# Attention with bias on one core: k and q transposed by the DMA engines, V in a ring of five pairs

## The chip, the core and the metric

The kernel runs on one core of a Trainium2 chip. Its engines work side by side, each with its own queue of instructions: PE (TensorE, matmuls and weight loads), DVE (VectorE), ACT (ScalarE), POOL (GpSimd) and SP (SyncE). Here POOL issues the loads and SP the stores. 16 DMA engines move the data for all queues. The metric is device time in microseconds (us); a run is one execution, and the time given is the median of several.

## What is computed

q, k and v are float32 arrays of shape 4 x 8 x 1024 x 64 (batch, heads, sequence, head dimension), the bias is 1 x 1 x 1024 x 1024 and is shared by all heads:

```python
scale = 1.0 / np.sqrt(head_dim)
scores = scale * np.matmul(q, k.transpose(0, 1, 3, 2))
scores = scores + bias
scores_max = np.max(scores, axis=-1, keepdims=True)
attn = np.exp(scores - scores_max) / (np.sum(np.exp(scores - scores_max), axis=-1, keepdims=True) + 1e-8)
return np.matmul(attn, v)
```

That is 32 heads, each with 1024 x 1024 scores, so 33.5 million exponentials.

## The kernel before

**Pairs, banks and groups.** Two heads make a pair, and there are 16 pairs (`NP`). A sequence of 1024 is cut into 8 chunks of 128 keys (`kc`) and two halves of 512 queries (`qh`). A *bank* is one block of transposed scores, 128 keys by 512 queries of one head; a pair has 32. `banks` (L113 to L146) is the order of all banks, in which the late banks of one half are mixed with the early banks of the next. Six banks are left out of that order (`dgroups`, L138 to L141): their exponential is computed on DVE in steps (`d_steps`, L205). All others are taken three at a time as a *group* (`slots`, L149): one activation of 128 x 1536 elements.

**The way of a bank.** `s_fill` (L165) writes a group's scores into a PSUM buffer `ps`, of which there are two: one matmul a bank (L172), with the transposed keys `kT` as weights and the transposed queries `qT` as the moving operand. Both heads share one `kT`: head 0 lies in partitions 0 to 63 and head 1 in 64 to 127, so `qT` holds each head's queries with zeros in the other half. `s_exp` (L178) takes the group through ACT's exp into a tile `E`. The bias comes in by multiplication on DVE with exp(bias), `eb` (`mul_pair`, L235); for the last two key chunks of the second query half it is added on PE instead, by a matmul with the identity (L176, the *late bias*), from `braw`, which DVE copies out of PSUM (L255). `av_bank` (L261) multiplies `E` with V and a column of ones into a small PSUM tile `po` (L269), over the 8 banks of one half of one head; then DVE takes the reciprocal of the sums (L279), scales (L281), and SP stores (L289).

**Loads and transposes.** `load_qk` (L75) loads k and q of a pair from HBM on POOL's queue, with a cast from float32 to bfloat16, into `kr` and `qr` (three buffers each). `load_v` (L82) loads V of a pair in two DMAs into `vall`, which holds all 16 pairs. `transpose_pe` (L86) transposes k or q on PE, 16 small transposes for a whole pair (L92), into a PSUM tile `px`; DVE then copies kT (L107) or multiplies qT with `mask`, which makes the zeros (L102). `kT` and `qT` have three buffers each (`kvp`). The tiles `px`, `po` and two others (`pd` and the late bias) share the two buffers of `ps_x`, named xa and xb.

**What sets the order.** Pair 0 is started by an order written out by hand (L324 to L404): the loads of pairs 0, 1 and 2, V of pairs 0 and 1 and the bias in four parts. The rest is laid out by a planner that runs when the program is built. It keeps a modelled time for ACT, DVE and PE, with a cost for each kind of work (`EXP`, `QK`, `AV`, `MUL`, `EVAC`, L409 to L410), and appends to each engine the piece of work that could start first. `pe_fill`, `pe_piece`, `pe_d` and `pe_av` offer work for PE, `dve_pick` for DVE from `dve_q`, a list of (due time, priority, cost, work), and `act_pick` for ACT. `raw_at` (L422) holds the times at which the planner believes that k and q of a pair have landed; it sets 26.0 and 28.5 us for pair 2, and 7 us from the issue for later pairs (L537). `pieces` (L424 to L429) lists the transposes of pairs 1 to 15; the one of q of a pair issues the loads of k and q three pairs on and of V two pairs on (L534 to L539). Within an engine the instructions then run in the order in which they were appended, and wait on semaphores for data and buffers.

Of the kernel before, what the change touches and what calls it, by code (L numbers as in the profile page):

```python
# [9 lines left out]
BF = mybir.dt.bfloat16  # L10
# [6 lines left out]
def kernel(  # L17
# [15 lines left out]
    nc = tc.nc  # L33
    B, H, S, D = q.shape
    P = 128
# [27 lines left out]
    eb = consts.tile([P, 2, NCH, HQ], BF)  # L63
    braw = consts.tile([P, 2, HQ], BF)
    mask = consts.tile([P, 2, HQ], BF)
    vall = consts.tile([P, 2 * NP, NCH, D1], BF)

    k0f = consts.tile([P, 2, QC, D], F32)
    q0f = [consts.tile([P, QC, D], F32, name=f"q0f{t}") for t in range(2)]
# [11 lines left out]

    def load_v(pr):  # L82
        for t in range(2):
            nc.gpsimd.dma_start(out=vall[:, 2 * pr + t, :, :D], in_=vf[pr, :, t])  # L84

    def transpose_pe(pr, which, c0, n, tag):  # L86

        src = raws[pr][which]
        px = ps_x.tile([P, n, P], BF, tag=tag, name="px")
        for c in range(n):  # L90
            for t in range(2):
                nc.tensor.transpose(px[t * D:(t + 1) * D, c, :], src[:, t, c0 + c, :], ident[:])  # L92
        if (pr, which) not in trs:
            trs[(pr, which)] = (kvp.tile([P, NCH, P], BF, name="kT") if which else
                                kvp.tile([P, 2, NCH * P], BF, name="qT"))
        dst = trs[(pr, which)]

        def copy():
            if which == 0:

                m = n // QC
                nc.vector.tensor_tensor(  # L102
                    dst[:, :, c0 * P:(c0 + n) * P].rearrange("p t (m q) -> p t m q", m=m),
                    px.rearrange("p (m c) q -> p m (c q)", m=m).unsqueeze(1).to_broadcast([P, 2, m, HQ]),
                    mask.unsqueeze(2).to_broadcast([P, 2, m, HQ]), op=ALU.mult)
            else:
                nc.vector.tensor_copy(dst[:, c0:c0 + n, :], px[:])  # L107
        return copy


    NE = NCH - 2
    DPR = (3, 7, 11)
# [52 lines left out]
    def s_fill(g):  # L165
        if ("S", g) not in open_ps:
            open_ps[("S", g)] = ps_s.tile([P, 3, HQ], F32, tag="s", name="ps")
        ps = open_ps[("S", g)]
        for j, b in enumerate(slots[g]):
            pr, h, qh, kc = banks[b]  # L170
            qT, kT = trs[(pr, 0)], trs[(pr, 1)]
            nc.tensor.matmul(ps[:, j, :], kT[:, kc, :], qT[:, h, qh * HQ:(qh + 1) * HQ],  # L172
                             start=True, stop=b not in late_bias)
        for j, b in enumerate(slots[g]):
            if b in late_bias:
                nc.tensor.matmul(ps[:, j, :], ident[:], braw[:, late_bias[b], :], start=False, stop=True)  # L176

    def s_exp(g):  # L178
        n = len(slots[g])
        nc.scalar.activation(e_at(slots[g][0], n), open_ps.pop(("S", g))[:, :n, :], ACTF.Exp, scale=scale)  # L180
# [6 lines left out]
    LOG2E = 1.4426950408889634  # L187

    def d_fill(b, tag):
        pr, h, qh, kc = banks[b]  # L190
        ps = ps_x.tile([P, HQ], F32, tag=tag, name="pd")
        nc.tensor.matmul(ps[:], trs[(pr, 1)][:, kc, :], trs[(pr, 0)][:, h, qh * HQ:(qh + 1) * HQ], start=True, stop=False)  # L192
        nc.tensor.matmul(ps[:], ident[:], braw[:, late_bias[b], :], start=False, stop=True)  # L193
        d = d_of[b][0]
        if d not in dtiles:
            dtiles[d] = {"y": dp.tile([P, 2, HQ], I32, name="dy"), "f": dp.tile([P, 2, HQ], F32, name="df"),
                         "p": dp.tile([P, 2, HQ], I16, name="dpw"),
                         "b": dp.tile([P, 2, HQ], F32, name="db"), "e": de.tile([P, 2, HQ], BF, name="de")}

        def fixed():  # L200
            nc.vector.tensor_scalar(dtiles[d]["y"][:, d_of[b][1], :], ps[:], scale * LOG2E * 65536.0, 127.0 * 65536.0,  # L201
                                    op0=ALU.mult, op1=ALU.add)
        return fixed
# [57 lines left out]
    def av_bank(b, tag):  # L261
        pr, h, qh, kc = banks[b]
        first, last = (b == units[pr, h, qh][i] for i in (0, -1))
        if first:
            po[h] = ps_x.tile([P, QC, D1], F32, tag=tag, name="po")
        acc = po[h]
        e = e_at(b, 1)
        for i in range(QC):
            nc.tensor.matmul(acc[:, i, :], e[:, 0, i * P:(i + 1) * P], vall[:, 2 * pr + h, kc, :],  # L269
                             start=(first and i == 0), stop=last, skip_group_check=True)  # L270
        if not last:
            return None

        def evac():
            if qh == 0:
                oalls[h] = op.tile([P, NCH, D], F32, tag=f"o{h}", name="oall")
            oall = oalls[h]
            rs = small.tile([P, QC, 1], F32, name="rs")
            nc.vector.reciprocal(rs[:], acc[:, :, D:D1])  # L279
            c0 = qh * QC  # L280
            nc.vector.tensor_tensor(oall[:, c0:c0 + QC, :], acc[:, :, :D],  # L281
                                    rs[:].to_broadcast([P, QC, D]), op=ALU.mult)
# [13 lines left out]
    def av_last(x, bs, tag):  # L296
        first = len(last_left[x]) == 8
        if first:
            po[x] = (ps_x if tag != "s" else ps_s).tile([P, M, D1], F32, tag=tag, name="po")
        acc = po[x]  # L300
        for b in bs:
            last_left[x].remove(b)
        for i in range(M):
            for b in bs:
                nc.tensor.matmul(acc[:, i, :], e_at(b, 1)[:, 0, (x * M + i) * P:(x * M + i + 1) * P],
                                 vall[:, 2 * NP - 1, banks[b][3], :], start=first and i == 0 and b == bs[0],
                                 stop=not last_left[x] and b == bs[-1], skip_group_check=True)
        if last_left[x]:
            return None

        def evac():
            oh = small.tile([P, M, D], F32, name=f"oh{x}")
            rs = small.tile([P, M, 1], F32, name=f"rh{x}")
            nc.vector.reciprocal(rs[:], acc[:, :, D:D1])
            q = (nc.scalar, nc.sync)[x]
            if x == 0:
                for i in range(M):
                    nc.scalar.activation(oh[:, i, :], acc[:, i, :D], ACTF.Copy, scale=rs[:, i, :])
            else:
                nc.vector.tensor_tensor(oh[:], acc[:, :, :D], rs[:].to_broadcast([P, M, D]), op=ALU.mult)  # L320
            q.dma_start(out=of[2 * NP - 1][:, QC + x * M:QC + (x + 1) * M, :], in_=oh[:])
        return evac

    with tc.manual_schedule():  # L324
# [10 lines left out]
        kr0 = raw.tile([P, 2, NCH, D], BF, name="kr")  # L335
        raws[0] = (qr0, kr0)
        kT0 = kvp.tile([P, NCH, P], BF, name="kT")
        qT0 = kvp.tile([P, 2, NCH * P], BF, name="qT")
        trs[(0, 0)], trs[(0, 1)] = qT0, kT0

        nc.gpsimd.memset(qT0[D:, 0, :HQ], 0.0)
# [53 lines left out]
        for x in range(2):  # L395
            for y in range(2):
                nc.vector.memset(mask[x * D:(x + 1) * D, y, :], 1.0 if x == y else 0.0)
        s_exp(2)
        load_v(0)
        nc.gpsimd.dma_start(out=btraw[:, QC:QC + 2, :], in_=bf_[:, QC:QC + 2, :])  # L400
# [21 lines left out]
        raw_at = {0: (5900, 12600), 1: (19600, 20900), 2: (26000, 28500)}  # L422
        PM = 2
        pieces = [(0, 0, QC, QC)]  # L424
        for pr in range(1, NP):
            if pr < PM:
                pieces += [(pr, 1, 0, QC), (pr, 0, 0, QC), (pr, 1, QC, QC), (pr, 0, QC, QC)]
            else:
                pieces += [(pr, 1, 0, NCH), (pr, 0, 0, NCH)]  # L429
# [66 lines left out]
        def pe_piece():  # L496
# [23 lines left out]
            def emit(t):  # L520
# [5 lines left out]
                def run(t2):  # L526
# [7 lines left out]
                    if pr < NP and which == 0 and c0 + n == NCH:  # L534
                        if pr + 3 < NP:
                            load_qk(pr + 3)
                            raw_at[pr + 3] = (t2 + 7000, t2 + 7000)  # L537
                        if pr + 2 < NP:
                            load_v(pr + 2)  # L539
                dve_q.append((t + pe_cost(t, cost_t) + SEM, 0, cost, run))  # L540
            return ready, cost_t, emit

# [4 lines left out]
        def act_bank():  # L547
            i = min(len(filled), NO - 1)
            while order[i][0] != "S":
                i -= 1  # L550
            return slots[order[i][1]][0]

        def pe_d():
            if not d_todo:
# [172 lines left out]

        while len(act_end) < NO or av_next < NA or any(last_left) or dve_q:
            c = []
            a, d, p = act_pick(), dve_pick(), pe_pick()  # L730
            if a:
                c.append((a[0], 0))
# [62 lines left out]
```

## Time and profile before

| | |
|---|---|
| median of 3 runs | 246.78 us (245.88 to 246.88) |
| profiled execution: its own time | 248.31 us |
| profiled execution: span from first to last instruction | 246.5 us |
| mean granted TensorE clock | 0.993 |
| DMA: mean rate | 97 GB/s, 23.80 MB in 48752 packets |

The profile is that of one execution. In its lines, an instruction is named by its line in the kernel, its engine and operation, and what it writes and reads (out<-in); "x170" is a count, then come the time in which the group kept its engine busy, the mean length of one, and the idle time of the engine just before them with what ended most of it. PE is the matmuls and PEld the weight loads. Where instructions overlap on one engine, the busy time is less than the count times the mean. The chain of waits follows the work back from the last instruction, at each step to what released it. In stretches, each engine has its busy time and, in brackets, how many instructions started there.

The kernel's time is made of a start of some 10 us (loads and transposes of pair 0, four activations that make exp(bias) between the first groups), the 16 pairs, and an end of some 5 us. PE ran 488 transposes of `kr` and `qr` at L92 in bursts of 16 (0.57 us a burst), DVE 16 copies of kT and 17 of qT.

### The profile page before, as it was taken

The page shows a single profiled execution, that of the slowest core. Times are in us where ns is not written, and L with a number is a line of the kernel's source. Part 1 is how long each engine was busy: PE and PEld are TensorE (multiplying, and loading weights), DVE is VectorE, ACT ScalarE, POOL GpSimd, SP SyncE. Part 2 cuts the span into 40 slices and gives each one's busy share as a digit, 9 for nine tenths or more (in the row PEclk, how much of TensorE's full clock was granted, in tenths as well). Part 3 has the DMA queues.
Part 4 walks back from the last instruction along what each step waited for, and adds up shares of the span by engine and source line. Part 5 has one row for each costly group of instructions (what it writes and reads, how often), then busy time and mean ns, then how long its engine had stood idle before and what let it go on. Part 6 is the DMA issues. An engine that isn't in the chain of part 4 may idle for free.

```text
span 246.5 us, 7234 instructions
## 1 busy us (share of the span) xinstructions
PE 229.9 (93%) x3154; PEld 144.8 (59%) x3207; DVE 219.2 (89%) x366; ACT 236.7 (96%) x181; POOL 55.3 (22%) x76
## 2 busy tenths in 40 slices
PE   8667999999999999999988999999998999999993
PEld 3244656665566656666654665666664566766653
DVE  2417799998999999999999999999999999999994
ACT  5599999999999999999999999999999999999993
POOL 7654333501441304140134000601500000000000
PEclk9799999999999999999999999999999999999999
DMA  5999995995689479492394920792911020202022
GB/s 113 179 197 193 192 131 102 148 84 122 65 123 160 51 122 121 107 116 80 56 127 91 82 88 25 114 122 75 140 45 45 1 88 4 86 1 88 35 77 65
DMA packets 48752, 23.80 MB, mean 97 GB/s; under 512 B 34512, under 2 KB 44624, under 8 KB 48720
## 3 DMA queue, kind: packets, MB, share of 16 engines
q0 software_dynamic: 42560, 14.42, 53.6%
q1 hardware_dynamic: 5872, 8.72, 9.8%
q8 instruction: 25, 0.41, 0.7%
q10 hardware_dynamic: 288, 0.20, 0.3%
q14 instruction: 7, 0.06, 0.1%
HBM read 29.36 MB, written 8.39 MB: 153 GB/s over the span
## 4 chain that ended last, share of the span: by engine, by line
ACT 45%; PE 44%; DVE 4%; DMA 2%; issue 2%; POOL 1%; ACTq 0%; POOLq 0%
ACT E L180 42%; PE ps L172 24%; PE po L269 13%; PE px L92 3%; PE ps L176 3%; ACT eb L232 3%; DMA kr<-in_k_dram 2%; DVE qT L102 1%; DVE E L242 1%; DVE E L239 1%; PE pd L192 1%; PE pd L193 1%; DVE oall L281 1%; DVE db L215 0%; DVE dy L201 0%
## 5 line engine op out<-in xcount | busy, mean ns | idle before, releaser
L180 ACT ACTIVATE E<-ps 128x1536 bf16<-128x1536 f32 (+1 forms) x170 | 227.9, 1525 | 2.8 <-PE ps L172 2.7
L172 PE MATMUL ps<-qT,kT 128*128 128x512 bf16 x454 | 134.9, 382 | 8.2 <-ACT E L180 3.3
L269 PEld LDWEIGHTS <-E 128*128 128x128 bf16 x1992 | 78.9, 98 | 34.1 <-DVE E L242 2.5
L269 PE MATMUL po<-vall,E 128*128 128x65 bf16 x1992 | 84.8, 194 | 0.8 <-DVE E L245 0.3
L242 DVE TENSOR_TENSOR E<-E,eb 128x2048 bf16<-128x2048 bf16 x60 | 72.4, 1217 | 0.0
L245 DVE TENSOR_TENSOR E<-E,eb 128x1024 bf16<-128x1024 bf16 x98 | 64.0, 683 | 4.2 <-ACT eb L232 4.0
L172 PEld LDWEIGHTS <-kT 128*128 128x128 bf16 x506 | 44.9, 97 | 36.6 <-issue 10.2
L84 POOL DMA_DIRECT2D vall<-in_v_dram x32 | 28.7, 902 | 7.1 <-DMA btraw<-in_bias_dram 3.5
L281 DVE TENSOR_TENSOR oall<-po,rs 128x256 f32<-128x256 f32 x63 | 26.7, 425 | 2.2
L78 POOL DMA_DIRECT2D kr<-in_k_dram x15 | 10.5, 699 | 64.5 <-PE px L92 62.4
L102 DVE TENSOR_TENSOR qT<-px,mask 128x2048 bf16<-128x2048 bf16 (+1 forms) x17 | 19.2, 1127 | 5.6 <-PE px L92 5.4
L79 POOL DMA_DIRECT2D qr<-in_q_dram x15 | 10.7, 716 | 48.2 <-PE px L92 47.2
L176 PE MATMUL ps<-braw,ident 128*128 128x512 bf16 x57 | 21.4, 378 | 0.1
L279 DVE RECIPROCAL rs<-po 128x4 f32<-128x4 f32 x63 | 11.2, 178 | 3.3 <-PE po L269 2.5
L107 DVE COPY kT<-px 128x1024 bf16<-128x1024 bf16 (+1 forms) x16 | 10.4, 652 | 0.8 <-PE px L92 0.8
L92 PEld LDWEIGHTS <-qr 128*64 128x64 bf16 x248 | 7.5, 109 | 5.4 <-issue 5.1
L92 PEld LDWEIGHTS <-kr 128*64 128x64 bf16 x240 | 7.2, 109 | 5.0 <-issue 4.7
L92 PE MATMUL px<-ident,qr 128*64 128x128 bf16 x248 | 10.2, 222 | 0.0
L92 PE MATMUL px<-ident,kr 128*64 128x128 bf16 x240 | 9.7, 222 | 0.0
L176 PEld LDWEIGHTS <-ident 128*128 128x128 bf16 x58 | 5.6, 97 | 6.9
L232 ACT ACTIVATE eb<-pb 128x2048 bf16<-128x2048 bf16 (+1 forms) x4 | 6.7, 1676 | 0.0
L226 PEld LDWEIGHTS <-btraw 128*128 128x128 bf16 x56 | 4.0, 146 | 2.0 <-issue 1.6
(59 smaller groups left out, 65.7 us busy)
## 6 DMA issues: line engine op xcount, KB each, us to landing
out_dram<-oall SPq DMA_DIRECT2D x28, 256.0 KB, 2.0
vall<-in_v_dram POOLq DMA_DIRECT2D x32, 128.0 KB, 5.5
kr<-in_k_dram POOLq DMA_DIRECT2D x15, 256.0 KB, 4.3
qr<-in_q_dram POOLq DMA_DIRECT2D x15, 256.0 KB, 4.7
btraw<-in_bias_dram POOLq DMA_DIRECT2D x4, 512.0 KB, 8.7
out_dram<-oall SPq DMA_DIRECT2D x7, 128.0 KB, 1.8
k0f<-in_k_dram SPq DMA_DIRECT2D x2, 128.0 KB, 3.0
q0f<-in_q_dram ACTq DMA_DIRECT2D x1, 128.0 KB, 2.6
```

What stands on the lines that cost most here:

```text
L84: nc.gpsimd.dma_start(out=vall[:, 2 * pr + t, :, :D], in_=vf[pr, :, t])
L92: nc.tensor.transpose(px[t * D:(t + 1) * D, c, :], src[:, t, c0 + c, :], ident[:])
L102: nc.vector.tensor_tensor(dst[:, :, c0 * P:(c0 + n) * P].rearrange("p t (m q) -> p t m q", m=m), px.rearrange("p (m c) q -> p m (c q)", m= ...
L172: nc.tensor.matmul(ps[:, j, :], kT[:, kc, :], qT[:, h, qh * HQ:(qh + 1) * HQ], start=True, stop=b not in late_bias)
L176: nc.tensor.matmul(ps[:, j, :], ident[:], braw[:, late_bias[b], :], start=False, stop=True)
L180: nc.scalar.activation(e_at(slots[g][0], n), open_ps.pop(("S", g))[:, :n, :], ACTF.Exp, scale=scale)
L232: nc.scalar.activation(eb[:, qh, :n, c0 * P:(c0 + 2) * P], open_ps.pop(("B", qh, c0))[:, :n].rearrange("p k c q -> p k (c q)"), ACTF.Exp)
L242: nc.vector.tensor_tensor(e, e, eb[:, qh, kc:kc + 2, :].unsqueeze(2).to_broadcast([P, 2, 2, HQ]), op=ALU.mult)
L245: nc.vector.tensor_tensor(e, e, eb[:, qh, kc:kc + 1, :].to_broadcast([P, n, HQ]), op=ALU.mult)
L269: nc.tensor.matmul(acc[:, i, :], e[:, 0, i * P:(i + 1) * P], vall[:, 2 * pr + h, kc, :], start=(first and i == 0), stop=last, skip_group_c ...
L279: nc.vector.reciprocal(rs[:], acc[:, :, D:D1])
L281: nc.vector.tensor_tensor(oall[:, c0:c0 + QC, :], acc[:, :, :D], rs[:].to_broadcast([P, QC, D]), op=ALU.mult)
```

## The change

Pairs 0 and 1 (`XP = 2`) are transposed as before. For pairs 2 to 15:

- `q_spread`, one DVE copy, spreads q of the pair into `qpad`: 33 column blocks of 64, in which the blocks with odd numbers take the 16 chunks of q (8 of each head) and the others stay zero. There are two such tiles, zeroed once by DVE in the start, behind the memsets of `mask`.
- `xbar` issues three DMA transposes on SP's queue, from SBUF to SBUF: all of `kr` into `kT` (8 blocks of 128 x 128, 256 KB), and `qpad` twice into `qz` (16 blocks, 512 KB each), once from column 64 on and once from column 0. A block of `kT` now holds two neighbouring key chunks of one head, the even one in partitions 0 to 63 and the odd one in 64 to 127; `qz` holds the queries of both heads in the lower half with zeros above, and in the upper half with zeros below. `qk` picks the operands accordingly. The number, shape and order of the score matmuls and of the exps are unchanged.
- `dve_xb` appends the spread of pair p once the fills have reached six banks into pair p - 2 and the raw data is due by the planner's time; the loads of pair p + 3 follow it.
- `vall` holds five pairs (`VR`). V of pair v is loaded from the planner's main loop once the fills have reached pair v - 2 and the po matmuls of pair v - 5 are all appended.

```diff
-    vall = consts.tile([P, 2 * NP, NCH, D1], BF)
+    VR = 5
+    vall = consts.tile([P, 2 * VR, NCH, D1], BF)
+    qpad = [consts.tile([P, 4 * NCH + 1, D], BF, name=f"qpad{i}") for i in range(2)]
...
-            nc.gpsimd.dma_start(out=vall[:, 2 * pr + t, :, :D], in_=vf[pr, :, t])
+            nc.gpsimd.dma_start(out=vall[:, 2 * (pr % VR) + t, :, :D], in_=vf[pr, :, t])
...
+    XP = 2
+
+    def q_spread(pr):
+        nc.vector.tensor_copy(qpad[pr % 2][:, :4 * NCH, :].rearrange("p (c w) d -> p c w d", w=2)[:, :, 1, :],
+                              raws[pr][0].rearrange("p t c d -> p (t c) d"))
+
+    def xbar(pr):
+        kT = kvp.tile([P, NCH, P], BF, name="kT")
+        qz = kvp.tile([P, 2, 2, NCH * P], BF, tag="qT", name="qz")
+        qp = qpad[pr % 2].rearrange("p c d -> p (c d)")
+        nc.sync.dma_start_transpose(out=kT[:], in_=raws[pr][1].rearrange("p t c d -> p (t c d)"))
+        for e in range(2):
+            nc.sync.dma_start_transpose(out=qz[:, e].rearrange("p t (c q) -> p (t c) q", q=P),
+                                        in_=qp[:, (1 - e) * D:(1 - e) * D + 4 * NCH * D])
+        trs[(pr, 0)], trs[(pr, 1)] = qz, kT
+
+    def qk(pr, h, qh, kc):
+        qT, kT = trs[(pr, 0)], trs[(pr, 1)]
+        q = slice(qh * HQ, (qh + 1) * HQ)
+        if pr < XP:
+            return kT[:, kc, :], qT[:, h, q]
+        return kT[:, h * QC + kc // 2, :], qT[:, kc % 2, h, q]
...
+        for x in range(2):
+            nc.vector.memset(qpad[x][:, ::2, :], 0.0)
         s_exp(2)
         load_v(0)
...
-        for pr in range(1, NP):
+        for pr in range(1, XP):
...
-                        if pr + 2 < NP:
-                            load_v(pr + 2)
...
+        def dve_xb():
+            nonlocal xb_next
+            pr = xb_next
+            if pr >= NP or pr not in raws or pr not in raw_at or act_bank() < first_of[max(pr - 2, 0)] + XLAG:
+                return
+            xb_next += 1
+
+            def run(t):
+                q_spread(pr)
+                xbar(pr)
+                for half in range(2):
+                    piece_end[(pr, 1, half)] = piece_end[(pr, 0, half)] = t + XBAR
+                if pr + 3 < NP:
+                    load_qk(pr + 3)
+                    raw_at[pr + 3] = (t + XBAR + 6000, t + XBAR + 6000)
+            dve_q.append((max(raw_at[pr]), 1, 420, run))
+
+        XLAG, XBAR = 6, 9000
+        v_next = 2
...
             c = []
+            dve_xb()
+            if v_next < NP and act_bank() >= first_of[v_next - 2] and av_next >= 4 * NCH * (v_next - VR + 1):
+                load_v(v_next)
+                v_next += 1
             a, d, p = act_pick(), dve_pick(), pe_pick()
```

More of the change, by code (lines that the diff above doesn't have):

```diff
@@ L94, in transpose_pe @@
             trs[(pr, which)] = (kvp.tile([P, NCH, P], BF, name="kT") if which else
-                                kvp.tile([P, 2, NCH * P], BF, name="qT"))
+                                kvp.tile([P, 2, NCH * P], BF, tag="qT", name="qT"))
         dst = trs[(pr, which)]
@@ L169, in s_fill @@
         for j, b in enumerate(slots[g]):
[L170 to L173, printed above, removed]
+            nc.tensor.matmul(ps[:, j, :], *qk(*banks[b]), start=True, stop=b not in late_bias)
         for j, b in enumerate(slots[g]):
@@ L189, in d_fill @@
     def d_fill(b, tag):
-        pr, h, qh, kc = banks[b]
         ps = ps_x.tile([P, HQ], F32, tag=tag, name="pd")
-        nc.tensor.matmul(ps[:], trs[(pr, 1)][:, kc, :], trs[(pr, 0)][:, h, qh * HQ:(qh + 1) * HQ], start=True, stop=False)
+        nc.tensor.matmul(ps[:], *qk(*banks[b]), start=True, stop=False)
         nc.tensor.matmul(ps[:], ident[:], braw[:, late_bias[b], :], start=False, stop=True)
@@ L268, in av_bank @@
         for i in range(QC):
-            nc.tensor.matmul(acc[:, i, :], e[:, 0, i * P:(i + 1) * P], vall[:, 2 * pr + h, kc, :],
+            nc.tensor.matmul(acc[:, i, :], e[:, 0, i * P:(i + 1) * P], vall[:, 2 * (pr % VR) + h, kc, :],
                              start=(first and i == 0), stop=last, skip_group_check=True)
@@ L305, in av_last @@
                 nc.tensor.matmul(acc[:, i, :], e_at(b, 1)[:, 0, (x * M + i) * P:(x * M + i + 1) * P],
-                                 vall[:, 2 * NP - 1, banks[b][3], :], start=first and i == 0 and b == bs[0],
+                                 vall[:, 2 * ((NP - 1) % VR) + 1, banks[b][3], :], start=first and i == 0 and b == bs[0],
                                  stop=not last_left[x] and b == bs[-1], skip_group_check=True)
@@ L337 @@
         kT0 = kvp.tile([P, NCH, P], BF, name="kT")
-        qT0 = kvp.tile([P, 2, NCH * P], BF, name="qT")
+        qT0 = kvp.tile([P, 2, NCH * P], BF, tag="qT", name="qT")
         trs[(0, 0)], trs[(0, 1)] = qT0, kT0
@@ L551, in act_bank @@
             return slots[order[i][1]][0]
+        xb_next = XP
+        def dve_xb():
[15 more added lines that the diff above has]
+        v_next = 2
         def pe_d():
```

## The prediction

> **What bounds the kernel now.** I read the page's busy shares first, then the chain of waits, then the stretches, then single instructions around the edit.
>
> ```profile
> PE 229.9 (93%) x3154; PEld 144.8 (59%) x3207; DVE 219.2 (89%) x366; ACT 236.7 (96%) x181; POOL 55.3 (22%) x76
> ...
> ACT 45%; PE 44%; DVE 4%; DMA 2%; issue 2%; POOL 1%; ACTq 0%; POOLq 0%
> ...
> L180 ACT ACTIVATE E<-ps 128x1536 bf16<-128x1536 f32 (+1 forms) x170 | 227.9, 1525 | 2.8 <-PE ps L172 2.7
> ```
>
> The chain names ACT and PE about equally, which invites the thought that relieving PE pays. The exp group says otherwise: 227.9 us for 170 exps is 1.341 us each (the mean of 1525 ns counts a start that overlaps the exp before), and they waited 2.8 us in all, 2.6 of it once, before 9.7 us. The stretches (columns: PE, PEld, DVE, ACT, POOL busy, clock, DMA share, GB/s) agree:
>
> ```profile
> 10.00:20.00 10.00, 6.88 (x54) 3.76 (x54) 1.15 (x2) 10.00 (x8) 6.42 (x10) 0.92 1.34 199
> 20.00:30.00 10.00, 9.19 (x111) 5.96 (x113) 8.21 (x17) 10.00 (x9) 2.99 (x5) 1.00 1.55 189
> 30.00:45.00 15.00, 14.73 (x191) 8.89 (x194) 14.56 (x26) 15.00 (x12) 5.82 (x8) 1.00 0.98 124
> ...
> 210.00:240.00 30.00, 29.24 (x440) 19.59 (x447) 28.77 (x52) 30.00 (x23) 0.00 (x0) 1.00 0.16 59
> ```
>
> ACT is busy in every microsecond from 9.7 to 241.7. I also took the ends of all exps from the trace: they stand 1.343 us apart for a full group of three banks, and what exceeds that comes to 0.46 us over the whole run. So the time is 9.7 (start) + ACT's string of exps + 4.8 (end). The change leaves the number and size of the exps as they are. Hence a **ceiling for the gain of about 0.4 us**, while every wait that reaches ACT is added in full and never won back.
>
> **What goes.** For 14 pairs PE loses 32 transposes (two bursts of 0.57 us) and DVE a kT copy of 684 ns and a masked qT copy of 1219 ns: 16 us of PE, 27 us of DVE. Both lie beside ACT, so they count for at most the 0.4 us above. ps_x's two buffers are no longer shared with transposes; same answer.
>
> **What comes, cheap parts.** Two memsets of qpad (544 words each; a 512-element memset took 0.38 to 0.49 us in the mask row) stand behind the mask memsets, which end at 10.5; DVE then idles 4.95 us until 15.4. Cost 0; without that gap 1 us. The V ring moves loads on POOL's queue (below); V of a pair waits for the po matmuls of the pair five before, over by three pairs, so 0, and the k and q loads queued behind it have 40 us. The q spread (128x1024 bf16, SBUF to SBUF) has no row: below, the 128x512 copy from PSUM took 0.42 us; above, the 128x1024 one 0.68. I take 0.45; 14 of them are 6 us on a DVE that is given back 27.
>
> **First wait: the spread of pair 3.** Reading the order of the changed kernel's instructions shows what the diff hides. The planner believes pair 3's q is there at 22 us and pair 2's at 28.5, so DVE gets the spread of pair 3 first, right after the first oall (L281), ahead of the second braw copy (L255). And POOL now issues the two V loads of pair 2 ahead of pair 3's k and q. Before:
>
> ```profile
> 18.47 0.71 POOL L78 DMA_DIRECT2D kr<-in_k_dram  x1 [1.66 <-ACT E L180]
> 19.78 0.71 POOL L79 DMA_DIRECT2D qr<-in_q_dram  x1 [0.60 <-DMA kr<-in_k_dram]
> 20.80 0.89 POOL L84 DMA_DIRECT2D vall<-in_v_dram  x1 [0.31 <-DMA qr<-in_q_dram]
> 24.30 0.88 POOL L84 DMA_DIRECT2D vall<-in_v_dram  x1 [2.61 <-DMA btraw<-in_bias_dram]
> ```
>
> Time from issue to landing of pair 3's q and of the second V, from the DMA view in windows of 1 us:
>
> ```profile
> qr<-in_q_dram POOLq DMA_DIRECT2D x1, 256.0 KB, 11.1
> ...
> vall<-in_v_dram POOLq DMA_DIRECT2D x1, 128.0 KB, 8.6
> ```
>
> So q of pair 3 landed at 30.9 and the V behind it at 32.9: 11 us of queue, landings 1.0 to 1.4 us apart. With V first, q takes V's place: the same semaphore that held V until 24.3 (a bias load) holds q, and q lands last, at about 32.9. DVE reaches the spread at 28.9. Queued behind it:
>
> ```profile
> 28.90 0.68 DVE L245 TENSOR_TENSOR E<-E,eb 128x1024 bf16<-128x1024 bf16 x1
> 29.50 0.42 DVE L255 TENSOR_SCALAR braw<-px 128x512 bf16<-128x512 bf16 x1
> 29.84 0.68 DVE L102 TENSOR_TENSOR qT<-px,mask 128x1024 bf16<-128x1024 bf16 x1
> ```
>
> The braw copy frees the ps_x buffer that the next unit's po needs, and PE, in order, stands at that po:
>
> ```profile
> 30.47 0.53 PE L269 MATMUL po<-vall,E 128*128 128x65 bf16 x12
> 30.95 0.81 PE L172 MATMUL ps<-qT,kT 128*128 128x512 bf16 x3
> ```
>
> Before, 30.47 led to an exp that started at 32.09, 1.62 later. Now: 32.9 + 0.45 spread + 0.42 braw + 0.1 = 33.85, + 1.62 = 35.45, that is **3.3 us** of ACT (with 0.1 for its prefetch). Bounds: q landing at 30.9 as before gives 1.3; pair 3's k transpose, which starts when k lands and takes a share of the engines, may add one k load's 1.2, so 4.5.
>
> **Second wait: pair 2's transposes.** All stand on SP's queue, pair 3's three ahead of pair 2's. Pair 2's kT takes the buffer of pair 0, last read by the scores fill of banks 45 to 47, at 33.6 to 34.4 before, so 37.5 now. Its second q half is wanted by the fill of banks 66 to 68, at 43.1 before, so 46.4 now. Each pair is 256 + 512 + 512 KB, 1.31 MB. What a pair takes, T, has no row:
>
> ```profile
> q0 software_dynamic: 42560, 14.42, 53.6%
> q1 hardware_dynamic: 5872, 8.72, 9.8%
> ...
> out_dram<-oall SPq DMA_DIRECT2D x28, 256.0 KB, 2.0
> ```
>
> Below: SP's output stores, 8.72 MB in 9.8% of 246.5 us, 361 GB/s, T = 3.6. Above: V's 128-byte packets (32 ns each in the packet records), 10240 of them on 16 engines, T = 20.5. A row of a 128x128 bf16 block is 256 bytes, between the packets of 128 bytes (32 ns) and 512 (27 ns): 5120 x 30 ns / 16 = 9.6 us one at a time; the engines' share of 1.55 in the stretch from 20 to 30 says that packets overlap by that much, so **T = 6.2**, my value, nearest to those two rows.
>
> Pair 3's q transposes start at 33.4 (its spread's end) and end at 33.4 + 0.8T = 38.4; pair 2's follow: + 6.2, + 2.0 to land (the output row), + 2.5 for two k/q loads that interleave (landings 1.2 apart), is 49.1. Late by **2.7 us**; in general 1.8T - 8.5. At T = 3.6 none, at 14.3 17.2. After that pair p is wanted every 32 banks, 14.3 us, with transposes issued 26 us ahead (58 banks), so T below 14.3 costs no more. Output stores queue behind them on SP; oall has two buffers per head, 28 us, enough. POOL's k loads now wait for a transpose three pairs back; they have 40 us.
>
> Two pages of the Trainium skill disagree here. DMA: Bandwidth & Descriptors (Latency and other measured facts) gives the DMA transpose 261 GB/s; by that T would be 5.0, the second wait 0.5, the total about 250 (estimate). VectorE: DVE Perf Modes (The three transpose paths) gives 1309 ns for one 128x128 block by DMA against 390 on TensorE; 40 blocks a pair one after another would be 52 us, over 750 us in all (estimate), which speaks against the change. No row here decides.
>
> **Sum.** 246.8 + 3.3 + 2.7 - 0.4 = **252.4 us**. The profiled execution's span is 246.5 and its time 248.3, 1.5 above the median 246.78 of the runs; the waits are differences, so I add them to the median.
>
> **Rivals.** (a) *Transposes don't keep pace*, T above 14.3: SP's queue becomes the bound. For: V shows how badly 128-byte pieces go, and the loads already hold 53.6%. Against: stores go at 361 GB/s. At T = 20.5, pair 15 is ready at 33.4 + 4.5 + 13.8 x 20.5 = 321, wanted at 232: 338 us. (b) *Not slower*: q of pair 3 lands before DVE comes to it. It decides at 28.9 + about 1 of slack on PE; it needs the load 3 us earlier than V's 32.9, by V's packets not delaying it, and a T of 5 or less: pair 2 then starts at 34.2 and is late by T - 4.4, so at T = 5 the time is 246.8 - 0.4 + 0.6 = 247.0. Against: landings in queue order in every row from 25 to 34. (c) *PE or DVE relief speeds ACT*: capped at 0.46 us by the spacing, 246.3; a gain over 0.5% has no room. That the change doesn't do what it says is excluded: the order has 448 fewer transposes on PE and 42 on SP.
>
> **How the numbers follow.** The measurement can tell about 0.5%, 1.2 us, from no change. Case above with T from 3.6 to 14.3: 0.74, of which the time runs from 246.8 + 1.3 = 248.1 to 246.8 + 3.3 + 17.2 - 0.4 = 266.9. (a) 0.16. (b) 0.07 within 0.5%, 0.01 by luck beyond; (c) 0.02, of which 0.01 is faster by more. So slower 0.90, same 0.08, faster 0.02; range 248.0 to 266.9, with the likeliest part from 249 to 257.
>
> **What would show it.** Right: ACT idle for about 3 us near 33, DVE waiting on the DMA of qr just before; a second ACT gap near 46, PE waiting on a transpose into qz or kT; exps 1.343 apart elsewhere; SP's transposes about 6 us a pair. Wrong: ACT unbroken to 60 us (b); gaps at every pair, 14 times (a); a new gap at the end, where the last transposes lie 25 us ahead and I cost nothing.

## The result and the profile after

The changed kernel takes **264.03 us** (median of four runs, 263.78 to 269.21) against 246.83 us (245.88 to 246.90) for the kernel before: a ratio of 1.0703, interval 1.067 to 1.0736. It is slower by 17.2 us; 5.6 us were forecast. Here and below, ratios leave out executions well above the fastest ones of the same kernel, and the profile is of one of these, the execution that took 269.21 us, so its waits add up to more than the median lost.

The page of the changed kernel:

```profile
PE 219.8 (82%) x2714; PEld 132.7 (50%) x2759; DVE 205.0 (77%) x361; ACT 237.1 (89%) x181; POOL 54.7 (20%) x76
...
ACT 46%; PE 26%; DVE 13%; DMA 7%; issue 4%; SPq 2%; ACTq 0%
...
L203 ACT ACTIVATE E<-ps 128x1536 bf16<-128x1536 f32 (+1 forms) x170 | 228.2, 1529 | 23.9 <-PE ps L196 18.4
...
out_dram<-oall SPq DMA_DIRECT2D x28, 256.0 KB, 6.5
...
qz<-qpad SPq DMA_TRANSPOSE x28, 7.4
```

PE has 10 us less to do and DVE 14, and it does not help. ACT's exps take the same 228 us as before (227.9), but their idle time went from 2.8 to 23.9 us. The chain now holds 7% of DMA and 13% of DVE. An output store takes 6.5 us to land where it took 2.0: it goes out on the same DMA queue behind the transposes (the stores that SP issued from 55.9 us on moved their first packet at 62.2).

ACT's timeline (start, length, engine and line, count of instructions run together; in brackets the idle time ahead and what ended it):

```profile
34.46 1.45 ACT L203 ACTIVATE E<-ps 128x1536 bf16<-128x1536 f32 x1 [4.35 <-PE ps L199]
36.83 9.51 ACT L203 ACTIVATE E<-ps 128x1536 bf16<-128x1536 f32 x7 [0.92 <-PE ps L199]
54.51 1.45 ACT L203 ACTIVATE E<-ps 128x1536 bf16<-128x1536 f32 x1 [8.17 <-PE ps L196]
64.65 1.45 ACT L203 ACTIVATE E<-ps 128x1536 bf16<-128x1536 f32 x1 [8.69 <-PE ps L196]
67.03 8.39 ACT L203 ACTIVATE E<-ps 128x1536 bf16<-128x1536 f32 x6 [0.93 <-PE ps L196]
```

All of the loss lies between 30 and 67 us; ACT is unbroken from there to its tail. The first wait is 4.35 + 0.92 = 5.3 us, the second, in two parts, 8.17 + 8.69 + 0.93 = 17.8. The sum is 23.1. The start came 2.1 us earlier in this execution (the first full exp ended at 9.02 us, in the profile before at 11.16; the kernel `e6_vring` below, all of whose transposes are on PE, had 8.9, so this varies by execution), and 246.5 - 2.1 + 23.1 = 267.5 is the span of 267.4.

What stood behind each wait, on DVE and PE:

```profile
31.73 0.43 DVE L117 COPY qpad<-qr 128x1024 bf16<-128x1024 bf16 x1 [4.88 <-DMA qr<-in_q_dram]
```

```profile
32.54 0.53 PE L291 MATMUL po<-vall,E 128*128 128x65 bf16 x12 [4.05 <-DVE braw L277]
...
53.46 1.01 PE L196 MATMUL ps<-qz,kT 128*128 128x512 bf16 x2 [8.04 <-DMA qz<-qpad]
...
63.15 1.46 PE L196 MATMUL ps<-qz,kT 128*128 128x512 bf16 x3 [7.80 <-DMA qz<-qpad]
```

The first wait runs as foretold: DVE stands at the spread of pair 3 until its q lands, the braw copy is queued behind it, and PE stands at the po that needs its buffer. In the second, PE waits twice for pair 2's qz: for its first transpose at 53.5 and its second at 63.2. SP shows why it came so late (x2 is the two transposes of one q):

```profile
30.42 1.33 SPq L124 DMA_TRANSPOSE kT<-kr  x1
32.18 11.83 SPq L126 DMA_TRANSPOSE qz<-qpad  x2
44.14 4.68 SPq L124 DMA_TRANSPOSE kT<-kr  x1
48.94 6.92 SPq L126 DMA_TRANSPOSE qz<-qpad  x2
```

Pair 3's three held SP for 13.6 us and pair 2's for 11.7, and PE had the last of pair 2 only at 63.2, some 7 us after SP had issued it. I had put 6.2 us a pair.

### The profile page after: what moved, and what is told of

It is laid out like the page before. It is cut to its first block, busy times and chain, and to the rows that moved or that the text cites. A ratio compares the mean times of both kernels' runs of the same rounds, so it can differ in the third digit from the quotient of the medians.

```text
span 267.4 us, 6431 instructions
## 1 busy us (share of the span) xinstructions
PE 219.8 (82%) x2714; PEld 132.7 (50%) x2759; DVE 205.0 (77%) x361; ACT 237.1 (89%) x181; POOL 54.7 (20%) x76
## 4 chain that ended last, share of the span: by engine, by line
ACT 46%; PE 26%; DVE 13%; DMA 7%; issue 4%; SPq 2%; ACTq 0%
ACT E L203 45%; PE ps L196 13%; PE po L291 8%; DVE E L264 6%; DMA qz<-qpad 4%; DMA qr<-in_q_dram 3%; PE ps L199 2%; ACT eb L254 1%; DVE oall L303 1%; PE ps L373 1%; DVE E L267 1%; SPq L124 1%; DVE db L237 1%; DVE dy L236 1%; SPq L126 1%
## 5 line engine op out<-in xcount | busy, mean ns | idle before, releaser
L203 ACT ACTIVATE E<-ps 128x1536 bf16<-128x1536 f32 (+1 forms) x170 | 228.2, 1529 | 23.9 <-PE ps L196 18.4
L196 PE MATMUL ps<-qz,kT 128*128 128x512 bf16 x403 | 117.8, 382 | 29.5 <-DMA qz<-qpad 15.8
L291 PEld LDWEIGHTS <-E 128*128 128x128 bf16 x1992 | 80.9, 99 | 51.1 <-DVE E L264 11.5
L291 PE MATMUL po<-vall,E 128*128 128x65 bf16 x1992 | 89.1, 195 | 8.4 <-DVE braw L277 4.0
L267 DVE TENSOR_TENSOR E<-E,eb 128x1024 bf16<-128x1024 bf16 x112 | 74.2, 686 | 10.5 <-ACT E L203 5.3
L264 DVE TENSOR_TENSOR E<-E,eb 128x2048 bf16<-128x2048 bf16 x53 | 64.3, 1219 | 2.6 <-ACT E L203 2.5
L86 POOL DMA_DIRECT2D vall<-in_v_dram x32 | 28.1, 883 | 11.8 <-PE po L291 5.6
L303 DVE TENSOR_TENSOR oall<-po,rs 128x256 f32<-128x256 f32 x63 | 26.7, 424 | 2.2
L196 PE MATMUL ps<-qT,kT 128*128 128x512 bf16 x58 | 18.4, 403 | 3.6 <-ACT E L203 1.6
L117 DVE COPY qpad<-qr 128x1024 bf16<-128x1024 bf16 x14 | 5.9, 418 | 4.9 <-DMA qr<-in_q_dram 4.9
L248 PE MATMUL pb<-ident,btraw 128*128 128x128 bf16 x56 | 4.1, 225 | 1.1 <-ACT E L203 0.5
L261 DVE TENSOR_TENSOR E<-E,eb 128x1024 bf16<-128x1024 bf16 (+1 forms) x7 | 4.1, 611 | 0.7 <-ACT E L203 0.6
L223 DVE TENSOR_SCALAR dy<-pd 128x512 int32<-128x512 f32 x6 | 4.1, 692 | 0.5 <-PE pd L215 0.3
L104 DVE TENSOR_TENSOR qT<-px,mask 128x1024 bf16<-128x1024 bf16 x3 | 2.1, 686 | 2.8 <-PE px L94 2.8
```

Of the source, the lines that this page charges most:

```text
L86: nc.gpsimd.dma_start(out=vall[:, 2 * (pr % VR) + t, :, :D], in_=vf[pr, :, t])
L196: nc.tensor.matmul(ps[:, j, :], *qk(*banks[b]), start=True, stop=b not in late_bias)
L264: nc.vector.tensor_tensor(e, e, eb[:, qh, kc:kc + 2, :].unsqueeze(2).to_broadcast([P, 2, 2, HQ]), op=ALU.mult)
L267: nc.vector.tensor_tensor(e, e, eb[:, qh, kc:kc + 1, :].to_broadcast([P, n, HQ]), op=ALU.mult)
```

## Experiments

**My theory**: two waits at the start and nothing after; the first is the wait of DVE for pair 3's q, the second is pair 2's transposes behind pair 3's on a slow queue. **Rivals**: the cost is spread over all pairs (transposes or SP's queue), or comes with the V ring, or with the transposes' place on SP and not their pace. Ratios are to the kernel before on the same chip.

### The parts: V ring alone, pair 2 on PE, pairs 2 and 3 on PE

`e6_vring` is the kernel before with the ring of five pairs for V, all transposes on PE:

```diff
-    vall = consts.tile([P, 2 * NP, NCH, D1], BF)
+    VR = 5
+    vall = consts.tile([P, 2 * VR, NCH, D1], BF)
```

> The kernel before with the ring of five V pairs and V loaded from the main loop, transposes all on PE. My theory: the ring costs nothing by itself, 246 to 247.5 us. Rival, the moved V loads delay something at the start: 248 us or more.

Measured 246.54 us, ratio 1.0000 [0.9987, 1.0013]. The ring is free, within 0.3 us.

`e3_xp3` and `e4_xp4` are the changed kernel with the first three, and the first four pairs on PE:

```diff
-    XP = 2
+    XP = 3      # e3_xp3; 4 in e4_xp4
```

> Pair 2 is transposed on PE as before, DMA transposes begin with pair 3, whose spread stays at its early place. My theory: the wait at the spread stays (some 5 us), the wait at pair 2's scores goes, 250 to 253 us. Rival, crowding at every pair: 13 of 14 pairs remain, 263 us.

> Pairs 2 and 3 are transposed on PE, pairs 4 to 15 by DMA, first spread past 45 us. My theory: both waits go and the rest costs nothing, 246 to 248 us, with ACT unbroken from 10 us on. Rival, crowding at every pair: 12 of 14 pairs remain, 261 us. Rival, the lower clock of PE: no change of the clock by pairs 2 and 3, so again about 261 us.

`e3_xp3`: 250.60 us, 1.0186 [1.0135, 1.0236]. ACT's timeline has one wait and no other:

```profile
34.61 41.94 ACT L203 ACTIVATE E<-ps 128x1536 bf16<-128x1536 f32 x31 [4.81 <-PE ps L199]
```

`e4_xp4`: 245.73 us, 0.9991 [0.9956, 1.0026], with ACT unbroken:

```profile
25.70 213.59 ACT L203 ACTIVATE E<-ps 128x1536 bf16<-128x1536 f32 x159
```

These three take the change apart: twelve pairs by DMA and the ring cost nothing; adding pair 3 costs 4.9 us (250.60 - 245.73), adding pair 2 another 13.4 (264.03 - 250.60), each with an uncertainty of some 1 to 1.5 us by the intervals. The rival of a cost in every pair is out. So is a gain: with PE and DVE relieved in twelve pairs the time is the same.

### The first wait: V behind, pair 2 first

`e2_vlate` issues V of pair 2 behind k and q of pair 3:

```diff
-            if v_next < NP and act_bank() >= ...
+            if v_next < NP and (v_next > 2 or 3 in raws) and act_bank() >= ...
```

> Only V of pair 2 is moved behind k and q of pair 3 on POOL's queue, as it stood in the kernel before; pair 3 is still spread first. My theory: the wait at the spread shrinks by the 2 us that V took, the wait for pair 2's transposes stays, 261 to 263 us. Rival, the order of V is the cause of the first wait as a whole: 5 us less, 259 us.

Measured 262.05 us, 1.0628 [1.0599, 1.0657]. The time fell by 2 us, as expected. In the profiles the first wait went from 5.3 to 1.8 us; the second stayed (8.18 + 5.15 + 0.93). Counted from the first full exp, pair 3's q landed 2.0 us earlier, and PE's clock stayed at 1.00 after the shorter stop. So V ahead of q accounts for 3.5 of the 5.3 us by the profiles; the medians show 2.0.

`e1_due33` tells the planner that pair 3's q is late, so pair 2 is spread and transposed first:

```diff
-                            raw_at[pr + 3] = (t2 + 7000, t2 + 7000)
+                            raw_at[pr + 3] = (t2 + 7000, t2 + 7000) if pr else (33000, 33000)
```

> Only the planner's due time of pair 3's q is changed, to 33 us, so that DVE spreads pair 2 first and SP transposes pair 2 first. My theory (two waits at the start: DVE at the spread of pair 3, then PE at pair 2's transposes that queue behind pair 3's): both waits shrink to 3 us or less together, 247 to 251 us. Rival, the transposes and the loads crowd the DMA engines at every pair: 260 us or more, since as many bytes move.

Measured 254.15 us, 1.0316 [1.0283, 1.0349]: above the forecast and below the rival. The first wait is gone, and of the second 4.6 us are left at 42 to 50 us. A third had not been expected: 2.5 us at 63, where DVE waits to write `oall` (L303) because stores stood on SP behind transposes.

### The second wait: half the work, fewer loads, another order

`e5_halfq` leaves out one of the two q transposes of every pair, and its scores use the other's:

```diff
-        for e in range(2):
+        for e in range(1):
```

> The second DMA transpose of q is left out for all pairs, and the odd key chunks take the first copy, so the scores of odd chunks are those of other operands. A pair then moves 0.75 MB instead of 1.25 MB. My theory, a queue of transposes in the start that must drain: the wait for pair 2 shrinks from some 19 us to 5 to 10, total 252 to 259 us, the wait at the spread stays. Rival, each DMA transpose costs a fixed time to land: two fewer of five ahead of pair 2, but the same loads, 262 us or more.

Measured 256.73 us, 1.0414 [1.039, 1.0439]: the first wait is 3.18 + 0.92 us, the second 5.80 + 0.65. The second wait falls from 17.8 to 6.5 us in the profiles, and the time lies in the forecast. A fixed time for each transpose, as the rival priced it, is out; the run takes away bytes and transposes together, so it doesn't tell one from the other.

`e7_noloads` replaces k and q of pairs 4 to 6 by a tile of zeros, to take loads out of the stretch:

```diff
     def load_qk(pr):
+        if pr in (4, 5, 6):
+            raws[pr] = (fix, fix)
+            return
```

> The changed kernel without the loads of k and q of pairs 4, 5 and 6, which read a tile of zeros instead; all transposes stay, and V of pairs 3 and 4 is loaded earlier. If the loads that share the DMA engines stretch the transposes of pairs 3 and 2: the wait at pair 2's scores falls from some 19 us to 0 to 6, total 250 to 257 us. If the transposes are as slow by themselves: 262 us or more.

Measured 267.12 us, 1.0849 [1.0826, 1.0873], the wrong way. Between 28 and 52 us the load queue moved 2.13 MB, more than the changed kernel's 1.73: POOL was not held by `kr` any more, and loads of later pairs came forward. The second wait was 11.31 + 1.40 us. The run says nothing against loads as the cause, and nothing clean for it.

`e9_klast` turns the order on SP around, to see whether the landing of kT, which releases `kr` and so the next loads on POOL, is what slows the q transposes behind it:

```diff
-        nc.sync.dma_start_transpose(out=kT[:], in_=...)
         for e in range(2):
             nc.sync.dma_start_transpose(out=qz[:, e]..., in_=qp[...])
+        nc.sync.dma_start_transpose(out=kT[:], in_=...)
```

> The changed kernel with the order on SP turned: both transposes of q first, that of k last. In the profile the landing of a pair's k transpose frees kr, and POOL then loads k, q and V of later pairs just as the pair's two q transposes follow. If these loads are what stretches the q transposes: the wait at pair 2's scores falls from some 19 us to 5 to 12, total 251 to 258 us; the wait at the spread stays. If the transposes are slow for another reason: 262 us or more.

Measured 263.43 us, 1.0677 [1.0636, 1.0718], a miss. Pair 3's q transposes held SP as long as ever:

```profile
31.29 12.21 SPq L125 DMA_TRANSPOSE qz<-qpad  x2
```

and the second wait (14.63 + 0.71 us) now was for pair 2's kT, at the end of the queue. The release of `kr` is not needed for the slowness. One load that goes out at the same time is enough: q of pair 4, issued at 31.56 us, whose 256 packets were drawn out to 43.4 us. Pair 2's two q transposes, which had no load beside them, held SP for 5.16 us.

`e10_klast_due33` joins that order with pair 2 first:

```diff
         for e in range(2):
             nc.sync.dma_start_transpose(out=qz[:, e]..., in_=qp[...])
+        nc.sync.dma_start_transpose(out=kT[:], in_=...)
...
+                            raw_at[pr + 3] = (t2 + 7000, t2 + 7000) if pr else (33000, 33000)
```

> As e9, with pair 3's q due at 33 us as in e1, so that pair 2 is spread and transposed first. Both waits named so far have then lost their causes: 247 to 250 us. If a start with DMA transposes is too crowded in any order: 252 us or more, as in e1.

Measured 249.85 us, 1.0151 [1.0114, 1.0187], as expected: 2.63 + 0.71 us are left at 43, with three small waits of 0.3 to 0.7 between 158 and 174. That is still 3.6 us slower than the kernel before.

### No load beside the transposes

Whether loads were the cause was still open. `e13_hold` stops POOL's queue with a copy of two columns that has to wait for the last of pair 2's qz; k and q of pairs 4 and 5 follow, those of 6 and 7 after pair 4's spread (pair 4's no longer go out with the transposes of pair 1):

```diff
                 q_spread(pr)
                 xbar(pr)
+                if pr == 2:
+                    nc.gpsimd.tensor_copy(hold[:], trs[(2, 0)][:, 1, 1, NCH * P - 2:])
...
-                if pr + 3 < NP:
-                    load_qk(pr + 3)
+                for nx in {3: (), 2: (4, 5), 4: (6, 7)}.get(pr, (pr + 3,)):
```

> The changed kernel with every load on POOL's queue held, by a 2-column copy that reads the last of pair 2's qz, until pair 2's transposes have landed; then k and q of pairs 4 and 5 follow, those of 6 and 7 after the spread of pair 4. Between about 33 us and the landing no k, q or V load is issued. My theory (transposes crawl only because cast loads run beside them, 5.1 us a pair alone): pair 3's three take 5 to 6 us on SP, pair 2's too, the second wait shrinks from some 13.4 us to 0 to 2, the first of 4 to 5 stays: 250.5 to 254, if the later loads come in time. Rival (the transposes are slow in this stretch by themselves, for instance through the output stores, the engines' traffic on SBUF or the start of the queue): SP's 12 us for the first two q transposes stay, and the time stays at 260 or above, since the loads then come later still.

The time is 260.08 us, 1.0555 [1.0515, 1.0595], and its executions differ much (256.18 to 265.14). SP's timeline of the one profiled, of 256.18 us:

```profile
29.71 1.33 SPq L125 DMA_TRANSPOSE kT<-kr  x1
31.45 6.15 SPq L127 DMA_TRANSPOSE qz<-qpad  x2
37.73 1.23 SPq L125 DMA_TRANSPOSE kT<-kr  x1
39.07 6.02 SPq L127 DMA_TRANSPOSE qz<-qpad  x2
...
54.18 13.11 SPq L127 DMA_TRANSPOSE qz<-qpad  x2
```

This is the cleanest evidence of the study. The same two transposes take SP 6.0 to 6.2 us with no load issued beside them (pairs 3 and 2, about 7.4 us a pair with kT), and 13.1 with the loads back (pair 4, after POOL was let go at 47.2). The packets of one stretch, 42 to 44 us, by queue (packets, MB, share of 16 engines) and with a q transpose's time to landing, first in the changed kernel:

```profile
q0 software_dynamic: 315, 0.31, 98.5%
q1 hardware_dynamic: 212, 0.05, 25.4%
...
qz<-qpad SPq DMA_TRANSPOSE x1, 14.5
```

then in `e13_hold`:

```profile
q1 hardware_dynamic: 1181, 0.29, 130.9%
...
qz<-qpad SPq DMA_TRANSPOSE x1, 5.1
```

The packets of the loads (queue 0) take 98.5% of the 16 engines' time in that stretch (packets overlap, so a sum can pass 100%), and the transposes (queue 1) move 0.05 MB instead of 0.29. ACT waits in `e13_hold` for 2.47 us at 33 and 1.69 + 1.33 + 0.81 us between 44 and 51. The second wait is thus 3.8 us where the changed kernel's profile has 17.8, and the rival as it was put, that SP's 12 us stay without the loads, is out.

The time missed its 250.5 to 254 because the held loads came late themselves: DVE stood at the spread of pair 4 until its q landed, as it does at pair 3's in the first wait, and ACT waited another 3.2 us at 56 to 61.

```profile
53.72 0.43 DVE L118 COPY qpad<-qr 128x1024 bf16<-128x1024 bf16 x1 [3.05 <-DMA qr<-in_q_dram]
```

The profile is of the fastest of the four executions; what the others (259.05 to 265.14 us) lost beyond it is not shown.

`e14_hold_due33` joins the hold, moved behind pair 3's transposes, with pair 2 first:

```diff
+                if pr == 3:
+                    nc.gpsimd.tensor_copy(hold[:], trs[(3, 0)][:, 1, 1, NCH * P - 2:])
...
+                for nx in {2: (), 3: (4, 5), 4: (6, 7)}.get(pr, (pr + 3,)):
...
+                            raw_at[pr + 3] = (33000, 33000)
```

> As before, and the spread and transposes of pair 2 ahead of those of pair 3 (its due time set so), with the loads held behind pair 3's transposes, then pairs 4 and 5, then 6 and 7 after pair 4's spread. My theory: the first wait goes since pair 2's q landed by 27 us, the second goes since nothing runs beside the transposes: 246 to 249. Rival: the second wait of some 3 to 4 us that the due time alone left stays, 250 to 255.

Median 263.51 us, ratio 1.0436 [1.0385, 1.0486], with executions from 255.71 to 266.93 us, a miss of both. In its profile (258.55 us) the wait at 42 to 47 is 3.2 us. Pair 2's q transposes still had V beside them, issued at 24.5 and moving until 38, and held SP for 10.59 us; pair 3's, with no load, for 5.04. Then the held loads came late: DVE waited 5.34 us for pair 4's q, and ACT 5.97 at 55 to 61. Pair 4's q transposes, beside those loads, took 16.9 us on SP, and ACT waited 2.49 at 82 for them. Holding loads moves the collision; it does not end it.

`e15_after_again` is the changed kernel once more:

> The changed kernel once more, for a profile of an execution near its median of 264: the first wait 4 to 5.5 us, the second 12 to 15, nothing else over 0.5 us.

One run, 270.42 us, not near the median: 3.5 us for the first wait and 19.8 for the second, where the execution of 269.21 us had 5.3 and 17.8. The executions of this kernel lie between 263.8 and 270.4 us; those of the kernel before, beside the experiments, between 245.8 and 247.5. That it is the second wait that makes the difference to 264 us is likely, since it was the longer by far in both profiles, but no execution near 264 us has a profile.

### How much room the steady state has, and a faster version

`e11_xp4_extra` is `e4_xp4` with one more transpose of 512 KB for each pair, into a tile that nobody reads:

```diff
+        nc.sync.dma_start_transpose(out=spare[:], in_=qp[:, D:D + 4 * NCH * D])
```

> As e4 (pairs 2 and 3 on PE), with one more transpose of 512 KB for each of the 12 pairs, into a tile that nobody reads: 40% more to transpose. If the transposes have room between pairs (14.3 us a pair, some 10 used): 245 to 250 us. If they are at their pace already, 13 of 14.3 us: 12 pairs x 3 to 4 us less the lead of 26 us, 255 to 275 us.

Measured 272.73 us, 1.1065 [1.1007, 1.1124]. Its waits (in total, count, longest):

```profile
DVE oall L305 <- DMA out_dram<-oall: 31.4, 10, 8.5
ACT E L205 <- PE ps L198: 23.0, 16, 7.4
```

With 40% more bytes the steady state breaks, and it breaks at the stores: they stand behind transposes on SP, and DVE cannot write the next `oall`. In `e4_xp4` SP is at its limit already: from 83.9 to 185.6 us its transposes take 11.1 to 15.6 us a pair (2.88 + 9.54 for one, 2.03 + 11.46 for the next), about 1 us of stores comes on top, and SP goes from pair to pair in 14.5 us, where ACT takes 14.3. The transposes' lead hides it.

`e8_xp4_d6` spends what DVE is given back: pairs 0 to 3 on PE and twelve banks instead of six by DVE's own exp.

```diff
-    DPR = (3, 7, 11)
+    DPR = (3, 5, 7, 9, 11, 13)
```

> As e4_xp4 (pairs 2 and 3 on PE), with six pairs instead of three that give two banks to DVE's exp in steps, so ACT has six banks less: 6 x 0.448 = 2.7 us. If ACT alone sets the length: 243 us. If DVE, which gets 21 us more, becomes the bound: 246 us or more.

Measured 251.11 us, 1.0173 [1.0151, 1.0194]. DVE became the bound: it is busy for 34.5 of the 35 us from 200 to 235, and ACT waits 6.1 us at the end for `rh`, the last of DVE's work. Another 2.2 us, at 198, go back to DVE waiting 3.8 us for an output store on SP's queue. No version here beats the kernel before; `e4_xp4` equals it.

## Why the prediction was right in kind and wrong in size

**Bound and ceiling: right.** ACT's string of exps sets the time; relieving PE and DVE in twelve pairs gave 0.9991 [0.9956, 1.0026] (`e4_xp4`). The ceiling of 0.4 us was not seen, and is within that interval. In the changed kernel PE had 10 us less to do and DVE 14, where 16 and 21 (27 less 6) had been put down; why it is less was not followed up, and the time does not hang on it.

**Costs at nothing: mostly right.** The V ring is free (`e6_vring`). The spread took 0.418 us, with 0.45 taken. The gap that I did not expect at the end did not come. "Output stores queue behind them on SP; oall has two buffers per head, 28 us, enough" failed: it holds in the changed kernel, whose large waits lie elsewhere, but not in `e1_due33` (2.5 us), `e8_xp4_d6` (2.2 us) and `e11_xp4_extra` (31.4 us of DVE's time). I counted the distance between uses of a buffer, and not the stores' place on a queue that transposes hold for 11 to 16 us of a pair's 14.3 (`e4_xp4`).

**First wait: right in mechanism and place, 3.3 us forecast, 4.9 measured** (`e3_xp3` less `e4_xp4`), above the bound of 4.5. Two things were missing. Pair 3's q came later: in the changed kernel the spread started at 31.73 us, which is 33.9 by the clock of the profile before (2.1 us later), and 32.9 was taken. POOL had issued that load at 23.74, 25.9 by the same clock, and 24.3 was taken. (The forecast's sum 32.9 + 0.45 + 0.42 + 0.1 is 33.87 and not 33.85; nothing hangs on it.) And PE was slower after it had stood still. The stretches of the changed kernel (columns as before; the clock is the third number from the end):

```profile
28.00:32.00 4.00, 0.50 (x3) 0.10 (x1) 0.27 (x1) 2.11 (x2) 0.00 (x0) 1.00 1.72 184
32.00:36.00 4.00, 3.24 (x30) 1.97 (x31) 4.00 (x9) 1.45 (x1) 0.71 (x1) 0.66 1.86 179
36.00:40.00 4.00, 4.00 (x51) 2.48 (x51) 3.02 (x7) 3.17 (x3) 1.43 (x2) 0.91 0.91 63
```

The granted clock was 0.50 from 33.3 to 36.7 us, and ACT had a second, short wait of 0.92 us. In `e3_xp3` the clock fell before PE started again, and the slow matmuls lie within its one wait of 4.81 us. The forecast had no such term.

**Second wait: right in mechanism and place, wrong in size: 2.7 us forecast, 13.4 measured.** The step that failed is the last term of its sum, "+ 2.5 for two k/q loads that interleave". From the end of pair 3's spread to PE's start on the last of pair 2 the forecast had 15.7 us (33.4 to 49.1). `e13_hold`, without loads, took 15.6 (31.42 to 47.06); the changed kernel's profile 31.0 (32.16 to 63.15). So the loads cost some 15 us there, not 2.5.

The packet records split these 15 us. Far more loads ran than two: 1412 packets of k and q, at 256 packets a load five and a half loads, and 1872 of V, at 1024 a load nearly two. Some of them the lateness itself let in (k, q and two of V issued from 51.1 on, while pair 2's q was still moving). At the rates that such packets had by themselves (182 a us for k and q, `e13_hold`, 51 to 53 us; 1200 for V, `e2_vlate`, 30 to 31) that is an estimated 7.7 + 1.6 = 9.3 us. The other 6 us or so are what the mixture costs beyond the lengths. In part of the time the two queues go packet for packet, as in `e3_xp3` from 43 to 46 us:

```profile
q0 software_dynamic: 477, 0.46, 90.3%
q1 hardware_dynamic: 471, 0.12, 30.6%
```

A packet of a transpose is 256 bytes and one of a k or q load 1024, so the loads keep some 81% of the rate that they have by themselves (148 such packets a us; the count above holds 32 of 4 bytes), and the transposes 15% (157 a us, against 1070 at 49 to 51 us of the changed kernel). At 41 to 43 us of the changed kernel it was worse still: 73 packets of transposes a us, 7%, beside 106 of the loads, 58%.

T itself was not far off: 6.2, against 7.4 without loads (`e13_hold`) and 8.2 on average over pairs 5 to 15 of the changed kernel (6.4 to 13.6). That is partly luck. By themselves the packets took 18 to 19 ns and not 30, they overlapped by 1.24 (1070 x 18.6 ns / 16 engines) and not by 1.55, and there are pauses that the working does not have. It is luck too that all waits of `e13_hold` up to 51 us come to 6.3 us, near the 3.3 + 2.7 forecast: the first was 2.5, and the second 3.8 without the loads that the 2.7 had counted.

The pauses are the record's surprise. From 47 to 49 us of the changed kernel no load moved, and yet only 625 packets of transposes went, where 49 to 51 had 2204 (64 of them of 4 bytes): from 47.7 to 48.7 almost nothing moved. A 16 KB packet of the instruction queue (q8) had gone at 46.91. Over all sixteen runs there are 152 such packets with at least 200 packets of transposes in the microsecond behind them, and in 151 cases ten or more packets that started within 2 us took over 0.6 us each; of 42 that had only loads beside them, none. What links them no run tests.

The Trainium skill's rate of 261 GB/s (DMA: Bandwidth & Descriptors, Latency and other measured facts) agrees with the best stretches without loads (274 GB/s at 49 to 51 us of the changed kernel). Over two whole pairs without loads it was 168 GB/s (2.62 MB in 15.6 us, `e13_hold`), and 40 at 43 to 46 us of `e3_xp3`. Its 1309 ns for a block of 128 x 128 by DMA (VectorE: DVE Perf Modes, The three transpose paths) cannot be added up: 40 blocks took 7.4 us, not 52.

**Rivals.** (a), transposes that don't keep pace, was not seen in the changed kernel, where SP held 8.2 us a pair from pair 5 on and the loads mostly fell between the transposes (26% of the transposes' packets from 76 to 205 us went in half microseconds with five or more packets of loads). It was nearer than that looks: in `e4_xp4`, where that share is 48% from 83 to 186 us, SP went at 14.5 us a pair, against the threshold of 14.3, and 40% more work takes it over (`e11_xp4_extra`). (b) fell with the first wait, (c) with `e4_xp4`.

**What stays open.** That the loads beside the transposes cause most of the second wait is shown; the 6 us beyond their lengths are not explained. Packet for packet accounts for stretches like the one above, and not for those in which both crawl: at 39 to 41 us of the changed kernel 242 transpose packets and 43 load packets went in a us, 23 to 24% of the rate of either alone, the load packets at 252 ns each instead of 98. No run here tells what held both. Why executions of the changed kernel differ by 6 us is likewise not settled.

## What to carry to other kernels

Work that is moved to the DMA engines is to be priced in the stretch where it first has a deadline, beside all the loads that run until it is done, those that its own lateness lets in among them; its time alone is no guide, and adding the loads' lengths to it is not enough. Where a queue is given long transfers, ask which short ones now stand behind them, and which engine waits for those. And where one engine's string of work sets the time, relief of the others can only be spent if it buys that engine something: here the safe form (first four pairs on PE) is worth nothing that these runs can tell.

## What the runs showed of the hardware

- A transpose from SBUF to SBUF ran as packets of 256 bytes, for 256 KB and 512 KB alike. Half of them took 18 ns or less where nothing else moved (1070 a us at 49 to 51 us of the changed kernel) and 31 ns beside loads with a cast (157 a us in `e3_xp3`, 43 to 46; 73 in the changed kernel, 41 to 43).
- SP's queue was held while transposes went out: 6.0 to 6.2 us for two of 512 KB without loads (`e13_hold`), 11.8 (changed kernel, 32 us) and 16.9 (`e14_hold_due33`, 57 us) beside them. The output stores behind them waited for it.
- In 151 of 152 cases a packet of the instruction queue amid transposes was followed by a pause of packets over 0.6 us long; beside loads alone in none of 42.
- PE's granted clock went to 0.50 for 3.4 us at the first wait when PE had stood still for 3.0 to 4.05 us (`e5_halfq`, `e3_xp3`, changed kernel), and stayed at 1.00 there after 2.01 and 2.65 us (`e2_vlate`, `e13_hold`). In the changed kernel and `e5_halfq` a second wait of 0.92 us followed.
